# Batched 64x64 matmul: VectorE casts b, ScalarE evacuates seven of eight result blocks, and a is regrouped after its tile's multiplication

## The chip, the cores and the metric

The kernel runs on one core of a Trainium2 chip. The metric is the device time of one execution in microseconds; of several runs the median counts. A core has TensorE (PE in the profile; its weight loads are PEld), VectorE (DVE), ScalarE (ACT), GpSimd (POOL) and SyncE (SP), which run side by side and wait for each other through semaphores. Data go between the device memory (HBM) and the on-chip memory (SBUF) by DMA; transfers are issued from the queues of SP, ACT and POOL and share 16 DMA engines. Matmul results arrive in PSUM, and VectorE or ScalarE copies them out.

## The reference

```python
def setup_inputs():
    return {
        "a": np.random.randn(1024, 64, 64).astype(np.float32),
        "b": np.random.randn(1024, 64, 64).astype(np.float32),
    }

def reference(a, b):
    return np.matmul(a, b).astype(np.float32)
```

There are 1024 independent products of 64x64 matrices. Each of a, b and the output is 16.78 MB in float32.

## The kernel before

The batch is cut into 16 tiles of 64 products (index `t`, `n_t = 16`). Block `s` of a holds 128 products, two tiles, so there are 8 blocks. The whole order of work is written out by hand in one loop over `t` (under `manual_schedule`): each engine executes its instructions in the order in which the loop issues them. Buffers come from pools; an instruction that would overwrite a buffer waits until the last reader is done.

The steps, with their lines:

- `load_a` (L67) brings a block of a as four DMAs on POOL's queue, which turn float32 into bfloat16 on the way. Block 0 comes as float32 through SP and ACT (L82). There are four buffers.
- `load_b` (L88) brings a tile of b as float32 in one DMA of 1 MB, on SP's queue for even tiles and ACT's for odd ones. There are four buffers (`B_AHEAD = 4`), so tile `t + 4` can only be loaded when tile `t` has been cast.
- `regroup` (L99) copies a block of a on VectorE into another order, 128x4096 bfloat16 elements.
- `transpose` (L108) turns pairs of bfloat16 columns of it, seen as float32, on TensorE; ScalarE copies each result from PSUM to `at_sb` (L111), two copies per tile.
- `spread` (L121) copies on VectorE from `at_sb` into a block-diagonal operand `at_bd`, four copies of 32x1024 float32 per tile. There are two such operands.
- `cast` (L132) turns the tile of b into bfloat16, 128x2048 elements, on ScalarE. The last tile is cast in four quarters, two on ScalarE (L139) and two on VectorE (L137).
- `multiply` (L177) runs 64 matmuls per tile in two halves. Each half fills a PSUM tile `o_ps` (two of these exist, so a half waits for the copies of the same half one tile before), and `evacuate` (L165) copies it to `o_sb` in four pieces of 64x512: ScalarE takes the four pieces of the first half, VectorE the four of the second. The last tile uses smaller PSUM tiles and pieces of 64x256.
- `store` (L154) writes a tile of results, 1 MB, from POOL's queue, one tile late (`HOLD = 2`). Seven `o_sb` buffers exist.

One turn of the loop for tile `t` issues: spread and cast of tile `t + 1`; the load of b tile `t + 4`; on even tiles the regrouping of block `s + 2` and the load of block `s + 5`; the multiplication of tile `t` with its evacuation; a transposition for a later tile; the store of tile `t - 1`. In VectorE's queue of an even turn before the change this is: four spreads, one regrouping, four pieces of evacuation.

Of the kernel before, what the change touches and what calls it, by code (L numbers as in the profile page):

```python
# [13 lines left out]
def kernel(  # L14
# [14 lines left out]
    nc = tc.nc  # L29
# [4 lines left out]
    n_t, n_s = B // 64, B // 128  # L34
# [29 lines left out]
    def load_a(s):  # L64
        a_sb = a_pool.tile([128, 4, 16, 64], bf16, name="a_sb")
        for h in range(4):
            nc.gpsimd.dma_start(  # L67
                out=a_sb[:, h, :, :].rearrange("p v k -> p (v k)"), in_=a_v[s, h]
            )
        a_tiles[s] = a_sb  # L70

    def load_first_a():

        raw = [
            o_pool.tile([128, 8, 2, 2, 64], fp32, name="o_sb")[:].rearrange(
                "p gh j wl n -> p (gh j wl n)"
            )
            for _ in range(2)
        ]
        parts = [raw[h % 2][:, 1024 * (h // 2) : 1024 * (h // 2) + 1024] for h in range(4)]  # L80
        for h in range(4):
            (nc.scalar if h % 2 else nc.sync).dma_start(out=parts[h], in_=a_v[0, h])  # L82
        a_tiles[0] = parts

    def load_b(t):
        b_sb = b_pool.tile([128, 16, 128], fp32, name="b_sb")
        queue = nc.scalar if t % 2 else nc.sync
        queue.dma_start(out=b_sb[:], in_=b_v[t])  # L88
        b_tiles[t] = b_sb

    def regroup(s):
        a_sb = a_tiles.pop(s)
        a_bf = work.tile([128, 16, 4, 64], bf16, name="a_bf")
        if s == 0:
            for h in range(4):
                copy = nc.scalar.copy if h % 2 else nc.vector.tensor_copy
                copy(a_bf[:, :, h, :], a_sb[h].rearrange("p (v k) -> p v k", v=16))  # L97
        else:
            nc.vector.tensor_copy(a_bf[:], a_sb[:].rearrange("p h v k -> p v h k"))  # L99
        abf_tiles[s] = a_bf  # L100
        at_tiles[s] = work.tile([128, 2, 32, 2, 4, 4], fp32, name="at_sb")

    def transpose(s, j):
        a_cols = abf_tiles[s][:].rearrange("p v h k -> p v (h k)").bitcast(fp32)
        for wl in range(2):
            at_ps = t_psum.tile([128, 4, 128], fp32, name="at_ps")
            for vo in range(4):
                nc.tensor.transpose(  # L108
                    at_ps[:, vo, :], a_cols[:, 4 * vo + 2 * j + wl, :], identity[:]
                )  # L110
            nc.scalar.copy(  # L111
                at_tiles[s][:, j, :, wl, :, :],
                at_ps[:].rearrange("p vo (g mp) -> p g mp vo", mp=4),
            )

    def spread(t):
        half = slice(16 * (t % 2), 16 * (t % 2) + 16)
        bd = bd_tiles[t % N_BD]
        for h in range(4):
            rows = slice(32 * h, 32 * h + 32)  # L120
            nc.vector.tensor_copy(  # L121
                bd[rows, :, :, :, h, :].rearrange("p j g wl mo -> p j (g wl) mo"),
                at_tiles[t // 2][rows, :, half, :, :, :].rearrange(
                    "p j g wl mp vo -> p j (g wl) (mp vo)"
                ),
            )

    def cast(t):
        b_bf = work.tile([128, 16, 128], bf16, name="b_bf")
        b_sb = b_tiles.pop(t)  # L130
        if t < n_t - 1:
            nc.scalar.copy(b_bf[:], b_sb[:])  # L132
        else:
            for gq in range(4):
                rows = slice(4 * gq, 4 * gq + 4)
                if gq % 2:
                    nc.vector.tensor_copy(b_bf[:, rows, :], b_sb[:, rows, :])  # L137
                else:
                    nc.scalar.copy(b_bf[:, rows, :], b_sb[:, rows, :])  # L139
        bbf_tiles[t] = b_bf  # L140

    def store(t):
        for piece in held.pop(t):
            piece()

    def multiply(t):
        at_bd = bd_tiles[t % N_BD][:].rearrange("p j g wl h mo -> p j g (wl h mo)")
        at_bd = at_bd.bitcast(bf16).rearrange("p j g (c u) -> p j g c u", u=2)
        b_bf = bbf_tiles.pop(t)
        last = t == n_t - 1  # L150
        o_sb = o_pool.tile([128, 8, 2, 2, 64], fp32, name="o_sb")

        def put(lo, n):
            nc.gpsimd.dma_start(  # L154
                out=o_v[t, :, lo : lo + n, :],
                in_=o_sb[:, lo : lo + n].rearrange("p gh j wl n -> p (gh j wl n)"),
            )

        def evacuate(o_ps, gh, n, copy):

            for par in range(2):
                for wl in range(2):
                    src = o_ps[64 * wl : 64 * wl + 64, :, par, :, :]
                    dst = o_sb[64 * par : 64 * par + 64, gh : gh + n, :, wl, :]
                    copy(dst, src)  # L165

        for half in range(2):
            if not last:
                o_ps = o_psum.tile([128, 4, 2, 2, 64], fp32, name="o_ps")
            for g8 in range(8):  # L170
                if last and g8 % 4 == 0:
                    o_ps = t_psum.tile([128, 2, 2, 2, 64], fp32, name="at_ps")
                g = 8 * half + g8
                gl = (g8 % 4 if last else g8) // 2
                for j in range(2):
                    for u in range(2):
                        nc.tensor.matmul(  # L177
                            o_ps[:, gl, g % 2, j, :],
                            at_bd[:, j, g, :, u],
                            b_bf[:, g, 64 * u : 64 * u + 64],  # L180
                            start=(u == 0),
                            stop=(u == 1),
                        )
                if last and g8 % 4 == 3:
                    copy = nc.scalar.copy if g8 == 3 else nc.vector.tensor_copy
                    evacuate(o_ps, g // 4 * 2, 2, copy)
            if not last:
                copy = nc.vector.tensor_copy if half else nc.scalar.copy
                evacuate(o_ps, 4 * half, 4, copy)
        if last:  # L190
            held[t] = [lambda q=q: put(2 * q, 2) for q in range(4)]
        else:
            whole = t < n_t - 2
            held[t] = [lambda q=q: put(q, 8 if whole else 4) for q in ([0] if whole else [0, 4])]

    with tc.manual_schedule():
        load_first_a()

        nc.vector.memset(warm[:, 0:1], 0.0)
        nc.scalar.copy(warm[:, 1:2], warm[:, 0:1])  # L200
        for t in range(3):
            load_b(t)
        nc.vector.memset(bd_tiles[0][:], 0.0)  # L203
        make_identity(nc, identity)
        nc.gpsimd.memset(bd_tiles[1][:, 0], 0.0)  # L205
        load_a(1)
        nc.gpsimd.memset(bd_tiles[1][:, 1], 0.0)  # L207
        for s in range(2, A_AHEAD):
            load_a(s)
        regroup(0)  # L210
        transpose(0, 0)
        transpose(0, 1)
        load_b(3)
        spread(0)
        cast(0)
        regroup(1)
        load_a(A_AHEAD)
        transpose(1, 0)
        for t in range(n_t):
            s, half = t // 2, t % 2  # L220
            if t + 1 < n_t:
                spread(t + 1)
                cast(t + 1)
            if t + B_AHEAD < n_t:
                load_b(t + B_AHEAD)
            if half == 0:
                if s + 2 < n_s:
                    regroup(s + 2)
                if s + 1 + A_AHEAD < n_s:
                    load_a(s + 1 + A_AHEAD)  # L230
            multiply(t)
            if half == 0 and s + 1 < n_s:
                transpose(s + 1, 1)
            if half == 1 and s + 2 < n_s:
                transpose(s + 2, 0)
            if t >= HOLD - 1:
                store(t - HOLD + 1)
        for t in range(n_t - HOLD + 1, n_t):
            store(t)
# [30 lines left out]
```

## Time and profile before

| | |
|---|---|
| median of 7 runs | 137.26 us (136.58 to 138.58) |
| the profiled execution's own time | 136.58 us |
| its span in the profile | 134.5 us |
| VectorE busy | 106.7 us (79%) |
| ScalarE busy | 86.8 us (65%) |
| TensorE matmul busy | 67.0 us (50%) |
| GpSimd busy | 42.4 us (32%) |
| HBM read and written | 33.55 MB and 16.78 MB |

The span runs from the first to the last instruction of the profile; 2.1 us of the execution's time lie outside it. The page gives the busy time of every engine, the span cut into 40 slices with a digit of busy tenths each, the DMA rate in each slice, groups of equal instructions with count, total and mean time, and the idle time before them with what ended it. A stretch of the span can be asked for by itself; its row gives the busy time and count of each engine, the granted TensorE clock, the DMA share (mean busy share of the 16 DMA engines, which can read slightly above 1) and the rate. DMA rates count bytes as they are written: of the seven blocks of a that are converted on the way, only the bfloat16 half.

### The profile page before, as it was taken

The page shows a single profiled execution, that of the slowest core. Times are in us where ns is not written, and L with a number is a line of the kernel's source. Part 1 is how long each engine was busy: PE and PEld are TensorE (multiplying, and loading weights), DVE is VectorE, ACT ScalarE, POOL GpSimd, SP SyncE. Part 2 cuts the span into 40 slices and gives each one's busy share as a digit, 9 for nine tenths or more (in the row PEclk, how much of TensorE's full clock was granted, in tenths as well). Part 3 has the DMA queues.
Part 4 walks back from the last instruction along what each step waited for, and adds up shares of the span by engine and source line. Part 5 has one row for each costly group of instructions (what it writes and reads, how often), then busy time and mean ns, then how long its engine had stood idle before and what let it go on. Part 6 is the DMA issues. An engine that isn't in the chain of part 4 may idle for free.

```text
span 134.5 us, 2811 instructions
## 1 busy us (share of the span) xinstructions
PE 67.0 (50%) x1152; PEld 62.8 (47%) x1152; DVE 106.7 (79%) x145; ACT 86.8 (65%) x129; POOL 42.4 (32%) x56
## 2 busy tenths in 40 slices
PE   0006407930648352919670949194929494536400
PEld 0006307920628252909560939193919393536400
DVE  5950369008999999997999899989998989999940
ACT  3135426989077994684897597859785978972500
POOL 8981134114212441241134204140304031242460
PEclk9999975797579998685698686859595959995555
DMA  3999999999999999999999999999999999999693
GB/s 79 374 328 310 306 298 306 310 295 269 303 305 305 252 260 297 314 388 257 297 350 389 394 322 291 289 392 391 391 399 399 389 403 403 401 381 325 234 314 128
DMA packets 17484, 43.17 MB, mean 321 GB/s; under 512 B 1088, under 2 KB 1088, under 8 KB 17472
## 3 DMA queue, kind: packets, MB, share of 16 engines
q0 software_dynamic: 8448, 24.12, 61.8%
q1 hardware_dynamic: 4512, 9.44, 20.2%
q10 hardware_dynamic: 4512, 9.44, 18.5%
q8 instruction: 9, 0.15, 0.4%
q14 instruction: 3, 0.02, 0.0%
HBM read 33.55 MB, written 16.78 MB: 374 GB/s over the span
## 4 chain that ended last, share of the span: by engine, by line
DVE 39%; DMA 16%; PE 14%; issue 14%; POOL 9%; ACT 3%; POOLq 1%; ACTq 1%; DVEq 0%
DVE o_sb L165 24%; DMA a_sb<-in_a_dram 16%; PE o_ps L177 14%; DVE at_bd L121 14%; POOL out_dram L154 3%; POOL a_sb L67 3%; ACT o_sb L165 2%; POOL at_bd L207 1%; ACT b_bf L132 1%; POOL at_bd L205 1%; DVE a_bf L99 1%; POOLq L265 1%; ACTq L88 1%; POOL identity masks.py:199 0%; ACT at_sb L111 0%
## 5 line engine op out<-in xcount | busy, mean ns | idle before, releaser
L177 PEld LDWEIGHTS <-at_bd 128*128 128x128 bf16 x1024 | 45.8, 118 | 45.2 <-DVE o_sb L165 39.7
L177 PE MATMUL o_ps<-b_bf,at_bd 128*128 128x64 bf16 x960 | 44.3, 221 | 39.4 <-DVE o_sb L165 33.7
L121 DVE COPY at_bd<-at_sb 32x1024 f32<-32x1024 f32 x64 | 46.0, 719 | 7.7 <-ACT at_sb L111 5.7
L165 ACT COPY o_sb<-o_ps 64x512 f32<-64x512 f32 x60 | 34.8, 580 | 16.0 <-PE o_ps L177 15.5
L165 DVE COPY o_sb<-o_ps 64x512 f32<-64x512 f32 x60 | 41.3, 688 | 3.4 <-PE o_ps L177 2.6
L154 POOL DMA_DIRECT2D out_dram<-o_sb x20 | 20.1, 1004 | 51.5 <-DVE o_sb L165 20.0
L132 ACT CAST b_bf<-b_sb 128x2048 bf16<-128x2048 f32 x15 | 28.6, 1908 | 4.4 <-DMA b_sb<-in_b_dram 4.4
L108 PE MATMUL at_ps<-identity,a_bf 128*128 128x128 f32 x128 | 21.6, 326 | 17.4 <-ACT a_bf L97 11.4
L67 POOL DMA_DIRECT2D a_sb<-in_a_dram x28 | 18.3, 660 | 35.9 <-DMA a_sb<-in_a_dram 33.0
L108 PEld LDWEIGHTS at_ps<-identity,a_bf 128*128 128x128 f32 x128 | 17.9, 171 | 17.8 <-issue 17.8
L111 ACT COPY at_sb<-at_ps 128x512 f32<-128x512 f32 x32 | 17.7, 588 | 8.2 <-PE at_ps L108 8.0
L99 DVE COPY a_bf<-a_sb 128x4096 bf16<-128x4096 bf16 x7 | 8.6, 1227 | 8.3 <-DMA a_sb<-in_a_dram 8.1
L97 ACT CAST a_bf<-o_sb 128x1024 bf16<-128x1024 f32 x2 | 2.1, 1044 | 5.4 <-DMA o_sb<-in_a_dram 5.4
L165 ACT COPY o_sb<-at_ps 64x256 f32<-64x256 f32 x8 | 2.9, 366 | 3.5 <-PE at_ps L177 3.4
L177 PE MATMUL at_ps<-b_bf,at_bd 128*128 128x64 bf16 x64 | 3.6, 242 | 2.1 <-DVE at_bd L121 2.1
L97 DVE CAST a_bf<-o_sb 128x1024 bf16<-128x1024 f32 x2 | 3.2, 1623 | 1.5 <-DMA o_sb<-in_a_dram 1.4
L203 DVE MEMSET at_bd<- 128x4096 f32 x1 | 3.5, 3472 | 0.8 <-issue 0.8
L165 DVE COPY o_sb<-at_ps 64x256 f32<-64x256 f32 x8 | 3.4, 422 | 0.1
L200 ACT ACT_TABLE_LOAD x1 | 1.3, 1283 | 2.3 <-issue 2.3
L207 POOL MEMSET at_bd<- 128x2048 f32 x1 | 1.9, 1871 | 0.0
L205 POOL MEMSET at_bd<- 128x2048 f32 x1 | 1.8, 1799 | 0.0
L139 ACT CAST b_bf<-b_sb 128x512 bf16<-128x512 f32 x2 | 1.1, 618 | 0.0
(10 smaller groups left out, 2.5 us busy)
## 6 DMA issues: line engine op xcount, KB each, us to landing
out_dram<-o_sb POOLq DMA_DIRECT2D x14, 1024.0 KB, 21.5
a_sb<-in_a_dram POOLq DMA_DIRECT2D x28, 256.0 KB, 19.6
o_sb<-in_a_dram ACTq DMA_DIRECT2D x2, 512.0 KB, 7.4
o_sb<-in_a_dram SPq DMA_DIRECT2D x2, 512.0 KB, 6.1
out_dram<-o_sb POOLq DMA_DIRECT2D x2, 512.0 KB, 5.5
out_dram<-o_sb POOLq DMA_DIRECT2D x4, 256.0 KB, 3.5
b_sb<-in_b_dram SPq DMA_DIRECT2D x8, 0.5 KB, 15.9
b_sb<-in_b_dram ACTq DMA_DIRECT2D x8, 0.5 KB, 15.1
```

Source lines behind the costliest of these rows:

```text
L67: nc.gpsimd.dma_start(out=a_sb[:, h, :, :].rearrange("p v k -> p (v k)"), in_=a_v[s, h])
L97: copy(a_bf[:, :, h, :], a_sb[h].rearrange("p (v k) -> p v k", v=16))
L99: nc.vector.tensor_copy(a_bf[:], a_sb[:].rearrange("p h v k -> p v h k"))
L108: nc.tensor.transpose(at_ps[:, vo, :], a_cols[:, 4 * vo + 2 * j + wl, :], identity[:])
L111: nc.scalar.copy(at_tiles[s][:, j, :, wl, :, :], at_ps[:].rearrange("p vo (g mp) -> p g mp vo", mp=4),)
L121: nc.vector.tensor_copy(bd[rows, :, :, :, h, :].rearrange("p j g wl mo -> p j (g wl) mo"), at_tiles[t // 2][rows, :, half, :, :, :].rearrange(
L132: nc.scalar.copy(b_bf[:], b_sb[:])
L154: nc.gpsimd.dma_start(out=o_v[t, :, lo : lo + n, :], in_=o_sb[:, lo : lo + n].rearrange("p gh j wl n -> p (gh j wl n)"),)
L165: copy(dst, src)
L177: nc.tensor.matmul(o_ps[:, gl, g % 2, j, :], at_bd[:, j, g, :, u], b_bf[:, g, 64 * u : 64 * u + 64], start=(u == 0), stop=(u == 1),)
L203: nc.vector.memset(bd_tiles[0][:], 0.0)
L207: nc.gpsimd.memset(bd_tiles[1][:, 1], 0.0)
```

## The change

Three edits. In `cast`, every tile but the first and the last is cast by VectorE, not ScalarE. In `evacuate`, ScalarE takes all four pieces of the first half and three of the second, and VectorE only the last piece (`copies[3]`); the last tile stays as it was. In the loop, `regroup(s + 2)` is issued behind `multiply(t)` and no longer ahead of it.

```diff
-            nc.scalar.copy(b_bf[:], b_sb[:])
+            (nc.vector.tensor_copy if t else nc.scalar.copy)(b_bf[:], b_sb[:])
...
-        def evacuate(o_ps, gh, n, copy):
+        def evacuate(o_ps, gh, n, copies):
...
-                    copy(dst, src)
+                    copies[2 * par + wl](dst, src)
...
-                    evacuate(o_ps, g // 4 * 2, 2, copy)
+                    evacuate(o_ps, g // 4 * 2, 2, [copy] * 4)
             if not last:
-                copy = nc.vector.tensor_copy if half else nc.scalar.copy
-                evacuate(o_ps, 4 * half, 4, copy)
+                copies = [nc.scalar.copy] * 4
+                if half:
+                    copies[3] = nc.vector.tensor_copy
+                evacuate(o_ps, 4 * half, 4, copies)
...
             if half == 0:
-                if s + 2 < n_s:
-                    regroup(s + 2)
                 if s + 1 + A_AHEAD < n_s:
                     load_a(s + 1 + A_AHEAD)
             multiply(t)
+            if half == 0 and s + 2 < n_s:
+                regroup(s + 2)
             if half == 0 and s + 1 < n_s:
                 transpose(s + 1, 1)
```

VectorE's queue of an even turn is then: four spreads, one cast, one piece of evacuation, one regrouping.

## The prediction

> **What bounds the kernel now.** I read the page's slices first, then the groups, then single stretches, then the timeline at the start. The engines' busy shares and the slices:
>
> ```profile
> DVE  5950369008999999997999899989998989999940
> ...
> DMA  3999999999999999999999999999999999999693
> GB/s 79 374 328 310 306 298 306 310 295 269 303 305 305 252 260 297 314 388 257 297 350 389 394 322 291 289 392 391 391 399 399 389 403 403 401 381 325 234 314 128
> ...
> HBM read 33.55 MB, written 16.78 MB: 374 GB/s over the span
> ```
>
> Two things are full at once: VectorE from slice 10 (34 us) on, and the DMA engines from slice 1 until almost the end. Is DMA really a limit where it shows 300 GB/s? The rates count written bytes, 43.17 MB in all by the page, while 50.33 MB are read or written in HBM (50.5 with the instruction fetches). The missing 7.3 MB are the seven blocks of a that are halved on the way. So I count HBM bytes.
>
> ```profile
> 100.00:113.00 13.00, 8.90 (x144) 8.43 (x144) 11.82 (x17) 9.88 (x15) 2.58 (x2) 0.74 1.03 398
> 113.00:117.70 4.70, 3.01 (x96) 2.98 (x96) 4.52 (x8) 4.18 (x7) 1.35 (x1) 1.00 1.03 404
> 117.70:121.00 3.30, 1.24 (x37) 0.99 (x33) 3.19 (x5) 2.46 (x5) 1.38 (x2) 0.97 0.98 379
> 121.00:126.00 5.00, 3.59 (x64) 3.44 (x64) 4.83 (x9) 2.33 (x7) 0.78 (x1) 0.50 0.97 333
> 126.00:130.00 4.00, 0.00 (x0) 0.00 (x0) 3.30 (x8) 0.59 (x2) 3.17 (x5) 0.50 0.69 237
> 130.00:134.50 4.50, 0.00 (x0) 0.00 (x0) 0.00 (x0) 0.00 (x0) 0.42 (x1) 0.50 0.50 168
> ```
>
> The last two columns are DMA share and GB/s. From 117.7 us on, 379x3.3 + 333x5 + 237x4 + 168x4.5 = 4.62 MB move. So 45.9 MB went before, 0.27 of them in slice 0 (79 GB/s); the other 45.6 MB in the 115 us from 2.7 to 117.7: **397 GB/s, which is the rate of the best stretches (398 to 404)**. DMA was saturated all that time. Only the last 17 us are not: there few stores are outstanding, because VectorE finishes late. At 397 GB/s the 4.62 MB take 11.6 us, not the 14.7 until DMA falls silent near 132.4; after it 2.1 us pass to the span's end. A kernel that keeps DMA full to its end has a span of 117.7 + 11.6 + 2.1 = **131.4 us**. That is the floor: 3.1 us below 134.5, whatever the engines save.
>
> Here the Trainium skill speaks ("DMA: Bandwidth & Descriptors", Specifications): about 358 GB/s of HBM per core and a 435 GB/s fabric ceiling. By the first the bytes take 141 us and no gain is possible; by the second 116 us, and the span could fall to about 121. The trace's 397 lies between and decides.
>
> **The change part by part.** The rows with the durations (total, mean ns):
>
> ```profile
> L121 DVE COPY at_bd<-at_sb 32x1024 f32<-32x1024 f32 x64 | 46.0, 719 | 7.7 <-ACT at_sb L111 5.7
> L165 ACT COPY o_sb<-o_ps 64x512 f32<-64x512 f32 x60 | 34.8, 580 | 16.0 <-PE o_ps L177 15.5
> L165 DVE COPY o_sb<-o_ps 64x512 f32<-64x512 f32 x60 | 41.3, 688 | 3.4 <-PE o_ps L177 2.6
> ...
> L132 ACT CAST b_bf<-b_sb 128x2048 bf16<-128x2048 f32 x15 | 28.6, 1908 | 4.4 <-DMA b_sb<-in_b_dram 4.4
> ...
> L111 ACT COPY at_sb<-at_ps 128x512 f32<-128x512 f32 x32 | 17.7, 588 | 8.2 <-PE at_ps L108 8.0
> L99 DVE COPY a_bf<-a_sb 128x4096 bf16<-128x4096 bf16 x7 | 8.6, 1227 | 8.3 <-DMA a_sb<-in_a_dram 8.1
> ```
>
> VectorE per tile before: 4x0.719 + 4x0.688 + half of 1.227 = 6.24 us; tiles follow each other every 6.62 us (spreads at 60.22 and, eight tiles on, 113.16).
>
> *Evacuation*: VectorE loses 3x0.688 = 2.06 us a tile, ScalarE gains 3x0.580 = 1.74. *Cast*: ScalarE loses 1.91. VectorE's price isn't in the trace at this shape. Its dense quarter (128x512, L137) took 426 ns, a float32 copy of 1024 per row in its median after 80 us 684: 258 ns per 512 elements more, so 426 + 3x258 = 1.20 us. A cast of 1024 into a strided target (L97) took 848 ns, which would lead to 426 + 3x422 = 1.69. I take 1.23, near the dense row, and keep 1.20 and 1.69. Sums per tile: **VectorE 2.88 + 1.23 + 0.69 + 0.61 = 5.41; ScalarE 7x0.580 + 2x0.588 = 5.24** (5.41 before).
>
> *A wait is added.* In the program as built, VectorE's one piece waits for ScalarE's count at the seventh piece of that tile, which before it did not. The Trainium skill ("PSUM — Partial Sum Buffer", PSUM bank collisions raise a hardware error) says why: two engines must not read one bank and quadrant together. No run here shows that. Behind that piece in VectorE's queue stand the regrouping, the next spreads and the next cast, and the matmuls of the tile after wait for these. So a loop over two tiles arises: end of a piece, regrouping 1.23 (every second tile), spreads 2.84 to 3.09, cast 1.23, first half of the matmuls 1.1 to 1.8 (by the granted clock), seven pieces with gaps 4.1, semaphore 0.1, the piece 0.69: 11.3 to 12.2, I take **12.0 us for two tiles**. Without that wait VectorE's own sum, 5.5 with gaps, would hold. Before: 13.2 for two.
>
> *The regrouping moves.* At the start it held VectorE:
>
> ```profile
> 30.59 1.23 DVE L99 COPY a_bf<-a_sb 128x4096 bf16<-128x4096 bf16 x1 [6.92 <-DMA a_sb<-in_a_dram]
> ...
> 31.83 2.79 DVE L165 COPY o_sb<-o_ps 64x512 f32<-64x512 f32 x4
> ...
> 34.65 2.83 DVE L121 COPY at_bd<-at_sb 32x1024 f32<-32x1024 f32 x4
> ```
>
> Tile 0's second half waited behind it. Now tile 0 is out by 29.3; the regrouping still waits for the same DMA and ends at 31.8, then come spreads to 34.7 and the cast of tile 2 to 35.9. Its buffer's next load (b tile 6, SP's queue) thus starts at 35.9 instead of about 31.3; a loads, whose issue doesn't depend on it, fill DMA meanwhile, so nothing; without them up to 4.6 us. Multiplication of tile 4 can start at 35.9 + 12.0 = 47.9 (52.99 before). ScalarE's loads of b (odd tiles) stand ahead of an evacuation and wait for a VectorE cast that the matmuls need anyway: nothing. The transposition after the odd tile finds the regrouping done, since that tile's second half waits for the same VectorE piece and takes longer than 1.23.
>
> *POOL* issues the same DMAs in the same order. But the cast is a rule's business: "SBUF — State Buffer", Who interferes with whom, in the Trainium skill says that VectorE's two-port copies (SBUF to SBUF) and GpSimd lock each other out for whole instructions, and that GpSimd then can't write DMA descriptors. The trace shows it small:
>
> ```profile
> 93.82 1.36 POOL L154 DMA_DIRECT2D out_dram<-o_sb x1 [4.95 <-DVE o_sb L165]
> ...
> 94.73 0.95 DVE at_bd L121
> ```
>
> A store's issue took 1.36 us beside spreads, 0.9 elsewhere, and one spread 0.95 instead of 0.69. So 0.26 us of VectorE per store by the row; by the rule up to the whole 0.9. POOL is busy 32%, so its own delay is free. By the row the loop is 12.3 to 12.5 for two tiles, by the rule 13.
>
> *The sum.* From 47.9, ten tiles at 6.0 to 6.25 put tile 14 at 108 to 110 (116.7 before). But compute now meets DMA: a tile's evacuation needs the store of seven tiles earlier landed. Near 86 us, 33.4 MB have moved: all of a, b to tile 13 or so, hence stores 0 to 2 only, while tile 10 needs store 3, which fits at about 91. That costs 5 us there, and gives compute's end near 123 instead of 129. DMA by then has moved 48 MB and still has 2.5, so it stays full. Of the 6 us that compute gains, **the floor lets 3.1 through**: span 131.4, own time 131.4 + 2.1 = 133.5. The profiled execution was 0.68 below the median; with that back, **134.2 us**, -2.2%.
>
> **The rivals.** About 1% (1.4 us) is what a measurement here can tell from none.
>
> *A: DMA floor, as above*, 133 to 135 us. For it: 397 GB/s throughout. Against: nearly all gain must survive several waits.
>
> *B: hardly any gain.* The stores that are left at the end go few at a time; such stretches ran at 333 GB/s. If the last 4.6 MB go at that rate, they take 13.9 us, 2.3 more: 136.5. Or the loop costs 13.2 and only the start's gain remains, of which the tail loses half: about 136. Against: with 1 MB stores queued deep, 113 to 117.7 ran at 404.
>
> *C: slower, by VectorE's wait for ScalarE.* With a cast of 1.69, spreads of 3.09, matmul half 1.9 and locks of 0.9 for both stores, two tiles take 1.23 + 3.09 + 1.69 + 1.9 + 4.1 + 0.1 + 0.69 + 1.8 = 14.5. It decides from about 14.2, where ten tiles lose the start's 5 us. If ScalarE is also late for the first half by 1 us a pair, 15.5: 11.5 us lost, 5 won: about 143. For it: VectorE has little idle to give. Against: every term is at its end.
>
> **How the numbers follow.** A 0.62, B 0.20, C 0.18. A and a fifth of B are faster by over 1% (below 135.9): 0.66. The rest of B, 0.16, is within 1%. Slower: 0.18. The range runs from 132.0 (the best stretch's 404 GB/s throughout takes 2.2 us less) to 138.8, with B and the mild part of C. A's own range is 132 to 135.5.
>
> **What would show it.** The cast row on VectorE at 1.2 to 1.3 us; VectorE's pieces waiting for ScalarE; VectorE below 90% in the middle; multiplication of tile 4 near 48; waits for landed stores before evacuations around tile 10; DMA over 380 GB/s up to 126 us or later. Wrong would be: DMA falling under 350 in mid-kernel, or spreads 7 us or more apart per tile, which is C.

## The result, and the profile after

The changed kernel takes 136.13 us in the median of 24 runs, the kernel before 138.01 us in 61. The ratio is **0.9895, with a 95% interval of 0.9876 to 0.9915: 1.05% faster, just under half of the 2.2% that was forecast**. The ratio is formed from fast runs alone and leaves out those of the kernel before that took over 1.5% more than its fastest; the medians of all runs stand at 0.9864. The profiled execution took 135.93 us with a span of 134.1 us; the forecast for it was 133.5 and 131.4.

The page of the changed kernel, busy shares and rate in 40 slices:

```profile
DVE  5950359426996999699789943999149997995800
...
DMA  3999999999999999999999999999999999999991
GB/s 78 372 329 311 308 300 307 310 289 295 306 279 263 279 297 274 303 387 315 282 298 386 391 364 281 285 351 400 395 397 398 387 400 406 403 379 359 328 329 62
```

VectorE has holes now (slices 23 to 24 and 28 to 29), so it no longer bounds the kernel. DMA is busy to slice 38, where before it was only 6 tenths busy in slice 37. But the rate falls from about 400 to 330 in the last five slices although the engines stay busy. The groups that the change touches:

```profile
L165 ACT COPY o_sb<-o_ps 64x512 f32<-64x512 f32 x105 | 60.9, 580 | 23.5 <-PE o_ps L177 11.4
...
L165 DVE COPY o_sb<-o_ps 64x512 f32<-64x512 f32 x15 | 10.4, 694 | 18.3 <-ACT o_sb L165 18.1
...
L132 DVE CAST b_bf<-b_sb 128x2048 bf16<-128x2048 f32 x14 | 17.4, 1245 | 0.4
```

The cast costs 1245 ns on VectorE. The 15 single pieces are preceded by 18.1 us of waiting for ScalarE: the added wait is there. The stretches of the end, as for before (the last two columns are DMA share and GB/s):

```profile
113.00:117.70 4.70, 1.07 (x21) 1.08 (x22) 4.55 (x6) 4.29 (x8) 0.50 (x2) 0.82 1.03 404
117.70:121.00 3.30, 2.77 (x66) 2.65 (x64) 3.17 (x6) 2.39 (x5) 0.79 (x1) 0.73 1.03 379
121.00:126.00 5.00, 1.51 (x52) 1.39 (x48) 3.37 (x8) 4.59 (x11) 2.75 (x4) 1.00 1.01 351
126.00:130.00 4.00, 0.00 (x0) 0.00 (x0) 0.91 (x3) 0.00 (x0) 1.61 (x3) 0.54 0.99 322
130.00:134.10 4.10, 0.00 (x0) 0.00 (x0) 0.00 (x0) 0.00 (x0) 0.00 (x0) 0.50 0.29 108
```

Between 121 and 130 the DMA share is 0.99 to 1.01: the gaps are filled, as forecast. The rate of 322 to 351 is what was not; over 380 up to 126 us was the sign to look for. Lines of the timeline show how far ahead the engines are, and what holds them:

```profile
48.98 3.60 PE L177 MATMUL o_ps<-b_bf,at_bd 128*128 128x64 bf16 x64 [3.28 <-DVE b_bf L132]
...
78.40 2.96 ACT L165 COPY o_sb<-o_ps 64x512 f32<-64x512 f32 x5 [4.81 <-DMA out_dram<-o_sb]
...
94.82 2.95 ACT L165 COPY o_sb<-o_ps 64x512 f32<-64x512 f32 x5 [6.05 <-DMA out_dram<-o_sb]
...
123.45 3.48 DVE L165 COPY o_sb<-at_ps 64x256 f32<-64x256 f32 x8
```

Tile 4's multiplication starts at 48.98 instead of 52.99. Tiles 8 and 10 then wait for a landed store, 4.8 and 6.0 us. VectorE's last piece ends at 126.9 instead of 129.4.

### The profile page after: what moved, and what is told of

It reads as the page before. It is cut to its first block, busy times and chain, and to the rows that moved or that the text cites. A ratio compares the mean times of both kernels' runs of the same rounds, so it can differ in the third digit from the quotient of the medians.

```text
span 134.1 us, 2831 instructions
## 1 busy us (share of the span) xinstructions
PE 67.0 (50%) x1152; PEld 62.3 (46%) x1152; DVE 93.6 (70%) x114; ACT 87.1 (65%) x160; POOL 43.0 (32%) x56
## 4 chain that ended last, share of the span: by engine, by line
DMA 34%; issue 19%; DVE 17%; POOL 11%; ACT 9%; PE 4%; ACTq 1%; POOLq 1%; DVEq 0%
DMA out_dram<-o_sb 18%; DMA a_sb<-in_a_dram 17%; DVE at_bd L121 10%; ACT o_sb L165 9%; POOL out_dram L154 5%; DVE b_bf L132 4%; PE o_ps L177 4%; POOL a_sb L67 3%; DVE o_sb L165 3%; POOL at_bd L209 1%; POOL at_bd L207 1%; ACTq L88 1%; DVE a_bf L99 1%; POOLq L267 1%; POOL identity masks.py:199 0%
## 5 line engine op out<-in xcount | busy, mean ns | idle before, releaser
L165 ACT COPY o_sb<-o_ps 64x512 f32<-64x512 f32 x105 | 60.9, 580 | 23.5 <-PE o_ps L177 11.4
L177 PEld LDWEIGHTS <-at_bd 128*128 128x128 bf16 x1024 | 43.3, 114 | 39.3 <-DVE b_bf L132 26.6
L121 DVE COPY at_bd<-at_sb 32x1024 f32<-32x1024 f32 x64 | 47.0, 734 | 7.6 <-ACT at_sb L111 5.9
L108 PE MATMUL at_ps<-identity,a_bf 128*128 128x128 f32 x128 | 23.6, 348 | 20.0 <-ACT a_bf L97 11.1
L67 POOL DMA_DIRECT2D a_sb<-in_a_dram x28 | 19.8, 711 | 37.7 <-DMA a_sb<-in_a_dram 30.9
L108 PEld LDWEIGHTS at_ps<-identity,a_bf 128*128 128x128 f32 x128 | 19.8, 185 | 20.8 <-issue 17.8
L165 DVE COPY o_sb<-o_ps 64x512 f32<-64x512 f32 x15 | 10.4, 694 | 18.3 <-ACT o_sb L165 18.1
L132 DVE CAST b_bf<-b_sb 128x2048 bf16<-128x2048 f32 x14 | 17.4, 1245 | 0.4
L132 ACT CAST b_bf<-b_sb 128x2048 bf16<-128x2048 f32 x1 | 1.9, 1902 | 4.1 <-DMA b_sb<-in_b_dram 4.1
L177 PE MATMUL at_ps<-b_bf,at_bd 128*128 128x64 bf16 x64 | 2.0, 193 | 0.5 <-DVE at_bd L121 0.5
```

What stands on the lines that cost most here:

```text
L67: nc.gpsimd.dma_start(out=a_sb[:, h, :, :].rearrange("p v k -> p (v k)"), in_=a_v[s, h])
L108: nc.tensor.transpose(at_ps[:, vo, :], a_cols[:, 4 * vo + 2 * j + wl, :], identity[:])
L121: nc.vector.tensor_copy(bd[rows, :, :, :, h, :].rearrange("p j g wl mo -> p j (g wl) mo"), at_tiles[t // 2][rows, :, half, :, :, :].rearrange(
L132: (nc.vector.tensor_copy if t else nc.scalar.copy)(b_bf[:], b_sb[:])
L165: copies[2 * par + wl](dst, src)
L177: nc.tensor.matmul(o_ps[:, gl, g % 2, j, :], at_bd[:, j, g, :, u], b_bf[:, g, 64 * u : 64 * u + 64], start=(u == 0), stop=(u == 1),)
```

## The experiments

What had to be found was why the last megabytes go slower, and whether that is all that took the gain. Ratios are to the kernel before on the same chip, with their 95% interval.

### Which part of the change carries the gain

`e3_regroup_only`: the kernel before with this edit alone.

```diff
             if half == 0:
-                if s + 2 < n_s:
-                    regroup(s + 2)
...
             multiply(t)
+            if half == 0 and s + 2 < n_s:
+                regroup(s + 2)
```

> The kernel before with the regrouping behind the multiplication, and nothing else. By the prediction's sum VectorE keeps its 6.24 us a tile and only gains the start, where tile 0's second half waited for it: about 2.8 us earlier there, of which up to 1 us reaches the end (0 to 0.7% faster). Rival: the move alone brings all of the change's gain (1% faster).

Measured: 136.54 us, ratio 0.9947 (0.9913 to 0.9981), as expected. `e4_no_regroup` is the other half: the changed kernel with the regrouping back in its old place.

> The changed kernel with the regrouping put back ahead of the multiplication: cast and evacuation moved alone. If the exchange of work carries the gain, the time is within 0.3% of the changed kernel (1% faster than before). If the regrouping's place carries it, it is within 0.3% of the kernel before.

Measured: 136.10 us, ratio 0.9924 (0.9891 to 0.9958). It matches the changed kernel's 136.13; the intervals of e3 and e4 overlap, so the exchange of work is not shown to bring more than the move. **On top of the exchange of work, the move brings nothing that can be seen** (136.10 against 136.13 us), though alone it gains 0.5%. The ratios by themselves are too wide to show this: 0.9947 times 0.9924 is 0.9871, within the error of 0.9895. The stretches of e3 suggest why. With the move alone DMA is already nearly full at the end, at the same low rate:

```profile
117.70:121.00 3.30, 1.99 (x38) 1.83 (x36) 3.17 (x6) 1.10 (x2) 2.16 (x2) 0.50 1.02 374
121.00:126.00 5.00, 3.08 (x60) 2.96 (x57) 4.83 (x10) 2.93 (x8) 1.46 (x2) 0.71 0.96 334
126.00:130.00 4.00, 0.00 (x0) 0.00 (x0) 1.60 (x4) 0.00 (x0) 2.15 (x3) 0.66 0.99 327
```

### Do the engines still matter at all?

`e2_light` takes far more from VectorE than the change does: it leaves out three of a tile's four spread copies.

```diff
     def spread(t):
...
-        for h in range(4):
+        for h in range(1):
```

> The changed kernel with three of VectorE's four spread copies left out of every tile (about 2.1 us a tile; the output is not the reference's). Theory DMA floor: the engines are far ahead, DMA is full to the end, the time falls by no more than 1.5 us against the changed kernel and DMA's rate at the end is 330 to 350 GB/s. Theory compute: the engines still set the end, and the time falls by 5 us or more.

The page's busy times and rates of e2_light:

```profile
PE 67.9 (51%) x1152; PEld 63.4 (47%) x1152; DVE 55.4 (41%) x66; ACT 87.0 (65%) x160; POOL 46.1 (34%) x56
...
GB/s 88 362 328 311 306 301 305 311 294 294 306 300 267 305 287 299 305 328 386 341 300 305 336 405 289 234 389 390 397 394 383 401 398 402 407 362 350 339 331 56
```

VectorE is busy 55 instead of 94 us and done at 121.9, five us sooner. The time is 135.97 us (ratio 0.9912, 0.9878 to 0.9947), 0.16 below the changed kernel. So there is a floor for this order of transfers, and the changed kernel stands on it; but at 136 us and not at the 134.2 that the prediction had computed.

### Why is the end slow: place, time or queue?

In the trace's DMA packets one number changes: in the median a 4 KB packet of a store takes 165 to 169 ns until about 118 us, and from 123 us on about 189 ns. `e1_rot` asks whether it is the place in memory.

```diff
-                out=a_sb[:, h, :, :].rearrange("p v k -> p (v k)"), in_=a_v[s, h]
+                out=a_sb[:, h, :, :].rearrange("p v k -> p (v k)"), in_=a_v[(s + 4) % n_s, h]
...
-        queue.dma_start(out=b_sb[:], in_=b_v[t])
+        queue.dma_start(out=b_sb[:], in_=b_v[(t + 8) % n_t])
...
-                out=o_v[t, :, lo : lo + n, :],
+                out=o_v[(t + 8) % n_t, :, lo : lo + n, :],
```

> The changed kernel with the tiles of a, b and the output taken in rotated order (tile 8 of the batch first, tile 7 last); nothing else differs. In the changed kernel the 4 KB packets of the last stores take about 189 ns from 123 us on, before that 165. Theory address: the output's last 3 MB lie badly, so the slow packets move to the middle of the kernel (tiles 13 to 15 are now the sixth to eighth) and the last ones take 165 ns; the span falls by about 1.5 us or stays if the middle loses as much. Theory time (a long run of stores without loads, or something else at the end): the last packets stay at about 189 ns and the time within 0.3% of the changed kernel's.

Measured: 136.22 us, and the packets from 122 to 130 us again take 182 to 194 ns, those of the sixth to eighth tile 159 to 169. The place is not the cause. `e5_stores_pool` then measures stores by themselves:

```diff
+    tiles = [o_pool.tile([128, 8, 2, 2, 64], fp32, name="o_sb") for _ in range(2)]
+    for o_sb in tiles:
+        nc.vector.memset(o_sb[:], 1.0)
+    for t in range(n_t):
+        nc.gpsimd.dma_start(
+            out=o_v[t],
+            in_=tiles[t % 2][:].rearrange("p gh j wl n -> p (gh j wl n)"),
+        )
```

> Sixteen stores of 1 MB alone on POOL's queue, from two tiles that VectorE sets to one; no loads, no matmuls (the output is not the reference's). In the changed kernel stores without loads run at 400 GB/s for some 8 us and then fall to 325 to 350. Theory store limit (HBM takes writes alone at less than the mixed rate, behind something that holds a few MB): here too the rate is near 400 for the first 8 to 10 us, then 330 to 345 to the end; the stores take about 48 us. Theory queue end (only the last few stores in a queue are slow, because little is left in flight): 400 GB/s until the last two stores, about 42 us.

Its rates and bytes (40 slices of 1.5 us):

```profile
GB/s 0 0 0 223 351 265 320 337 329 329 331 326 329 331 326 326 331 337 329 326 329 331 320 334 334 326 320 334 329 334 326 334 331 329 343 337 290 209 173 0
...
HBM read 0.00 MB, written 16.78 MB: 285 GB/s over the span
```

**Stores alone run at 330 GB/s** in this one run, with many in the queue (packets mostly 196 to 200 ns). Neither theory of the expectation holds as it stood: it isn't only the last stores, but nor do these stores run at 400 for the first 8 us. The changed kernel's do, for some 8 us behind its last load. Both rates can be seen in its trace. From 111 to 121 us all traffic but an instruction fetch is stores (the rows are of queue, kind, packets, MB, share):

```profile
DMA packets 1015, 3.94 MB, mean 394 GB/s; under 512 B 57, under 2 KB 57, under 8 KB 1014
...
q0 software_dynamic: 1014, 3.92, 101.7%
```

And from 123.5 to 131 us:

```profile
DMA packets 682, 2.43 MB, mean 324 GB/s; under 512 B 92, under 2 KB 92, under 8 KB 680
...
q0 software_dynamic: 680, 2.41, 96.9%
```

The same kind of stores on the same queue: 394, then 324. What carries the 8 us was not found. That the missing loads are the cause was tested by putting some back, `e15_more_loads`:

```diff
-        queue.dma_start(out=b_sb[:], in_=b_v[t])
+        queue.dma_start(out=b_sb[:], in_=b_v[t % n_t])
...
-            if t + B_AHEAD < n_t:
+            if t + B_AHEAD < n_t + 2:
```

> The changed kernel with two more loads of b (tiles 0 and 1 once more, 2.1 MB, not used) behind the last. Mix theory: the stores' 4 KB packets keep 165 to 169 ns while these loads run and for some 8 us more, so the slow stretch starts near 128 instead of 123 us and the time rises by less than 5.3 us (2.1 MB at 397 GB/s), about 4.3. Rival (the last stores are slow by themselves): the packets of the stores from tile 13 on take about 189 ns beside the loads too, and the time rises by 5.3 to 6.4 us.

```profile
113.00:118.00 5.00, 0.00 (x0) 0.10 (x1) 3.48 (x4) 0.00 (x0) 0.39 (x1) 0.67 1.03 396
118.00:123.00 5.00, 1.09 (x21) 1.08 (x21) 0.00 (x0) 3.44 (x7) 0.00 (x0) 0.50 1.03 404
123.00:128.00 5.00, 3.09 (x56) 2.82 (x54) 4.16 (x7) 4.89 (x10) 1.54 (x2) 0.50 1.04 365
128.00:132.00 4.00, 3.15 (x60) 2.99 (x57) 3.48 (x8) 3.77 (x10) 2.08 (x4) 0.52 0.97 365
132.00:136.00 4.00, 0.00 (x0) 0.00 (x0) 1.07 (x3) 0.00 (x0) 1.77 (x3) 0.90 0.96 334
```

Measured: 140.54 us, 4.4 more than the changed kernel, where 4.3 was expected and 5.3 to 6.4 by the rival. The packets' median is 165 to 178 ns until 132 us; only from there on it is 187. The slow stretch has moved from 123 to 132 us, but the last load moved further, from 110.2 to 127.9: the stores stay fast for only some 4 us behind it. So the length of the fast stretch is no constant. While that last load runs beside few stores, the rate is 365 GB/s, less than in the mix before it.

Two further rivals: that the stores of the last two tiles are slow because they are cut into pieces of 512 and 256 KB is ruled out by `e8_o8` below, in whose trace whole 1 MB stores (tiles 11 to 13) already take 189 to 196 ns a packet in the median. That all stores go through one queue, POOL's, was not tested; the same queue carries 394 GB/s just behind the last load.

### Move the last load, and the time follows

If so, anything that makes loads end sooner should cost time, even if the engines get faster by it. `e8_o8` gives the results one buffer more (the first diff; `e11_o6` has `bufs=6` there); `e7_b3` takes one from b (the second).

```diff
-    o_pool = ctx.enter_context(tc.tile_pool(name="o_pool", bufs=7))
+    o_pool = ctx.enter_context(tc.tile_pool(name="o_pool", bufs=8))
```

```diff
-    B_AHEAD = 4
+    B_AHEAD = 3
...
-        load_b(3)
```

> The changed kernel with eight instead of seven result buffers. ScalarE's waits for landed stores (10.9 us in two waits) should fall by half or more, and the engines finish some 2 us earlier. Theory DMA end: the time stays within 0.3% of the changed kernel. Theory compute: it falls by 1 us or more.

> The changed kernel with six instead of seven result buffers, the opposite of the run with eight. Theory of the mix: the engines wait longer for landed stores, casts and so loads of b come later, less is stored behind the last load, and the time falls by 0.5 to 1.5 us although the engines wait more. Theory of engine waits: it rises by 0.5 us or more.

> The changed kernel with three instead of four buffers for b, each load issued one tile later, so that loads last longer and stores go earlier. If long runs of stores alone are what is slow, the run of stores at the end gets shorter by about one tile's time and the time falls by up to 1.5 us, unless a cast then waits for its load; each such wait is seen as VectorE waiting for b's DMA and costs nothing while DMA is full. If the slow end belongs to the last stores whatever went before, the time stays within 0.3% or rises.

The rates of e8_o8, and then of e7_b3:

```profile
GB/s 59 387 330 311 306 301 306 309 286 295 312 266 263 282 289 276 329 385 296 279 321 390 397 338 286 292 365 397 387 392 403 405 401 375 355 335 339 340 311 39
```

```profile
GB/s 58 377 335 311 306 293 274 257 269 304 306 260 270 297 277 291 386 350 278 282 366 387 392 316 305 287 387 400 395 395 388 399 398 392 402 404 403 372 335 41
```

With eight result buffers the rate falls seven slices before the end, with three b buffers three. ScalarE's wait for landed stores goes the other way: 2.5 us with eight, 10.9 with seven, 15.6 with six:

```profile
ACT o_sb L165 <- DMA out_dram<-o_sb: 15.6, 3, 7.3
```

The last load's packet and the bytes stored behind it, counted from the packets of each trace:

| kernel | last load packet, us | MB stored behind it | engines' last copy ends, us | median, us |
|---|---|---|---|---|
| e8_o8 | 105.7 | 9.57 | 121.0 | 137.58 |
| changed kernel | 110.2 | 7.70 | 126.9 | 136.13 |
| e11_o6 | 114.2 | 6.03 | 127.7 | 135.29 |
| e7_b3 | 115.3 | 5.74 | 125.5 | 135.09 |
| e14_b3_o6 | 117.5 | 4.78 | 127.7 | 135.01 |
| e2_light | 109.4 | 7.93 | 121.9 | 135.97 |

The order by bytes behind the last load is the order by time, except that e2_light is 0.16 us faster than the changed kernel at 0.2 MB more; the times of e11, e7 and e14 overlap. Of the runs not listed, e1, e4 and e9 have 7.55 to 7.71 MB and 136.07 to 136.22 us; e3, whose VectorE is busy to the end, has 7.90 MB and 136.54 us.

The size can be estimated: a megabyte at 330 instead of 397 GB/s takes 0.5 us longer. The 1.96 MB that e7 saves against the changed kernel make 1.0 us (measured 1.04), the 1.87 MB that e8 adds 0.95 (measured 1.45, so a part of e8 is not explained).

**Having the engines finish early buys nothing: e8's finish first of all, and it is the slowest.** For e8 the expectation of both theories was off: it lost 1.45 us against the changed kernel (ratio to before 0.9980, 0.9950 to 1.0011). e11 (0.9836, 0.9773 to 0.9899) and e7 (0.9815, 0.9772 to 0.9859) came as expected. Their sum, `e14_b3_o6`:

> The changed kernel with three buffers for b and six for results. Each alone moved the last load from 110.2 to 114 or 115 us and took 0.8 to 1.0 us. Mix theory: together the last load ends near 118 to 120 and less than 5 MB is stored behind it; the time falls another 0 to 0.7 us, to 134.4 to 135.2. Rival: with both the engines finish too late, DMA has gaps at its end and the time is above 135.5.

At 135.01 us (0.9787, 0.9718 to 0.9857) it is no different from e7 alone: the last load is later by 2.2 us, but now the end of the engines counts again, with a DMA share of 0.85 between 124 and 126 us. e7 is the simplest version that beats both kernels: 1.04 us below the changed one.

### Where later loads no longer help

`e10_b2` (two buffers for b), `e13_b3_a3` (three for b and for a, `A_AHEAD = 3`) and `e12_before_b3` (the kernel before with three for b):

> The changed kernel with two buffers for b, so that loads last still longer. Theory of the mix (stores alone run at 330 GB/s, stores beside loads at about 400): the last load lands near 120 us instead of 110, about 4 MB of stores are left behind it, and DMA ends some 1 us earlier than with three buffers, about 134 us in all. Rival: a load takes about 14 us and two tiles last 12.4, so VectorE's casts now wait for loads in every tile, the engines finish later than DMA needs and the time is 136 us or more.

> The changed kernel with three buffers each for b and a. The a loads are issued a tile pair later, behind more stores in POOL's queue. Mix theory: loads of a end later but those of b set the end, so the time stays within 0.3% of the run with three b buffers (135.1 us) or falls by up to 0.5 us. Rival: VectorE waits for a's blocks in mid-kernel and the time rises to 136 us or more.

> The kernel before with three buffers for b. Its DMA has gaps at the end because VectorE finishes late. By the mix theory less is stored alone, but VectorE's pace sets the last stores as before: the time falls by at most 0.7 us. If the buffers alone bring the gain that they bring to the changed kernel, it falls to about 136 us or less (1.3% or more).

Measured: 143.07, 135.32 and 142.11 us. e13 equals e7, as expected. e10 follows the rival, and e12 neither expectation. Waits of e10_b2, then of e12_before_b3:

```profile
DVE b_bf L132 <- DMA b_sb<-in_b_dram: 14.4, 6, 3.6
```

```profile
ACT b_bf L132 <- DMA b_sb<-in_b_dram: 26.3, 7, 5.8
```

In both the casts starve. In e12 a load on ScalarE's queue stands behind the cast of the tile two before it (one is issued at 52.16 us beside the cast of 52.08, which had itself waited for its data). That leaves two turns, 13 us, while a load took about 15 in the kernel before. In e7 the load is issued as soon as VectorE's cast of the tile three before has freed the buffer (46.64 us, behind the cast that ends at 46.56), and its own cast comes at 62.49, which leaves 15.9 us. By this reading it is the cast on VectorE that makes three buffers enough; shown are only the waits, not a run that removes them.

DMA is not idle while the casts of e10 starve; it is slow (slices of 3.5 us):

```profile
DMA  3999999999999999999999999999999999994494
GB/s 74 394 324 306 305 236 210 255 276 289 271 244 266 373 345 234 332 392 388 280 249 390 396 391 405 391 388 363 322 349 329 351 295 375 331 367 154 149 308 138
```

Within slices 28 and 29, from 101 to 103.5 us, the traffic is loads of b and hardly anything else: 276 GB/s at a share of 0.98. So it is not only stores that are slow alone: loads of b are too. By this reading casts that wait leave few stores to move, and the loads that they wait for get slower by it.

### The added wait

`e9_all_act` takes the wait away by giving ScalarE all eight pieces.

```diff
-                if half:
-                    copies[3] = nc.vector.tensor_copy
```

> The changed kernel with all eight pieces of a tile's evacuation on ScalarE, so that VectorE no longer waits for ScalarE's seventh piece. ScalarE then has 8x0.580 + 2x0.588 = 5.82 us a tile, VectorE 4.72. If the added wait set the changed kernel's pace of 12.4 us for two tiles, the pace becomes 11.6 to 12.0 in the stretch from 48 to 74 us. In both cases the time should stay within 0.3% of the changed kernel by the DMA theory; by a theory in which the pace counts it falls by about 1 to 2 us.

Two turns of VectorE's spreads in its timeline, four tiles apart:

```profile
48.57 2.84 DVE L121 COPY at_bd<-at_sb 32x1024 f32<-32x1024 f32 x4
...
72.31 3.65 DVE L121 COPY at_bd<-at_sb 32x1024 f32<-32x1024 f32 x4
```

Four tiles in 23.7 us are 11.9 for two, against 24.8 and 12.4 in the changed kernel (49.67 to 74.49). So two tiles take half a microsecond less. That is not the wait's price alone: a piece has moved to ScalarE as well, and VectorE now waits 2.2 to 2.7 us per two tiles for ScalarE's copies to `at_sb`. The time, 136.07 us (0.9887, 0.9841 to 0.9933), is the same. On the floor this pace costs nothing.

## Why the prediction was half right

- **The bound** was right in kind: DMA is the limit, and engine time beyond the floor is worth nothing (e2_light, e9_all_act). Case A's mechanism happened.
- **The step that failed is the tail's term in the sum**: the bytes left at 117.7 us at 397 GB/s. The forecast had 4.62 MB in 11.6 us. The changed kernel moves 379x3.3 + 351x5 + 322x4 + 108x4.1 = 4.74 MB (0.3 us more at that rate). Its DMA is busy until near 131.4, 13.7 us instead of 11.9 (346 GB/s instead of 397): 1.8 us for the rate. From there to the end of the span it is 2.7 instead of 2.1 us, since a few packets trickle until 132.2: 0.6 more. 131.4 + 0.3 + 1.8 + 0.6 is the measured 134.1.
- **The rate was known and misread.** The prediction's own line for 121 to 126 us had 333 GB/s at a DMA share of 0.97: the engines were full, so the packets were slow and stores were not missing. The prediction took the whole end for gaps that a faster VectorE would fill. Rival B used the 333 GB/s and had 136.5 us, close to what came, but put it down to few stores in flight: the right rate for a wrong cause. I set it aside because stores queued deep ran at 404 until 117.7. Those 404 lay within 8 us of the last load. Stores alone are slow however many are queued (e5_stores_pool).
- **The engine side** came close. The cast cost 1.245 us (1.23), two tiles 12.4 us (12.0 to 12.5), tile 4's matmuls began at 49.0 (47.9). The wait for landed stores came at tiles 8 and 10 with 4.8 and 6.0 us (once, 5 us). The engines ended at 126.9 instead of about 123, which the DMA backlog covered.
- **Locks and the added wait** stayed small: spreads went from 719 to 734 ns in the mean. Case C did not come near.
- **The step to the median** was a constant 0.68 us. The changed kernel's median lies only 0.2 above its profiled execution; before's, over 61 runs, 1.4 above. The kernel before scatters from 136.3 to 139.2 us, the changed one from 135.8 to 136.8. So of the 1.9 us between the medians the two profiles show 0.65 (135.93 against 136.58). Why before scatters more was not found.

## What to carry to other kernels

When the DMA engines are full, count in the profile not only how much is left to move at the end, but of which kind: take the rate of the mix only for stretches that have the mix, and measure stores alone before assigning them a rate. A share near 1 at a low rate, with no converting loads in it, means slow transfers and not too few of them. Engines that run further ahead pull loads forward and leave more stores alone at the end; one buffer fewer for the loads then helped where one more for the results hurt. Two edits that fill the same gap need not add up.

## What the runs showed of the hardware

Stores from SBUF to HBM alone, on POOL's queue, ran at 330 GB/s here (e5), loads and stores together at 387 to 400 GB/s (slices 27 to 32 of the changed kernel's page). After the last load, stores kept about 400 GB/s for some 6 to 8 us (about 3 MB) and then fell to 320 to 350, in the changed kernel and in e1, e7 and e8 alike; in e15 they stayed fast for some 4 us only, and stores that had no loads before them were never fast. Loads of b with hardly a store beside them ran at 276 GB/s (e10, 101 to 103.5 us), though loads of a and b together, before the first store, kept 392 to 402 GB/s (bytes read in HBM, counted from the changed kernel's packets between 10 and 54 us). What the stores' reserve is, is open, and so is whether a second queue would change it.
